# A sum kept in vector memory, carried into four matmul banks in rounded halves, and scatters that take both row halves in one step

## The chip, the cores and the metric

The kernel runs on one core of a Trainium2 chip. The metric is the device time of one execution in microseconds (us); several executions are timed and their median is given. A separate execution is recorded by the profiler, and every duration in this text comes from that one.

## The reference, cut to what matters

Two layers on 256 tokens of width 1024 in float32. The change sits at the end of the second layer, in its mixture of experts:

```
logits = xt @ w_router + b_router
top_logit, top_idx = top_k(logits, 2);  gates = softmax(top_logit)
for each token and each of its 2 experts e:
    y += gate * (silu(x @ w_gate[e]) * (x @ w_up[e])) @ w_down[e]
out = x + g_f * rms_norm(y, g_post)
```

There are 8 experts of inner width 3584. Each expert's tokens are gathered, run through three matrices, and added back to their rows with their gate weights.

## The kernel before

All weights stream once from HBM in pages of 1 MB (128 partitions by 2048 columns), issued by SyncE in a fixed order and held in a ring of buffers; a new page is issued when TensorE (PE) or VectorE (DVE) has let go of an old one.

The expert stage works on eight **units**, one for each expert. Unit 0 is a fixed expert; units 1 to 7 are the others, ranked by how many tokens they got. Unit 1 is *wide* (192 tokens: a full tile of 128 and a packed tile of 64). Units 2 and 3 hold 128 tokens. Units 4 to 7 are *narrow*, 64 tokens each. For full tiles every weight piece is split by ScalarE (ACT, line 387) and DVE (line 390) into two rounded float32 parts (type fp32r: `whi`, `wlo`), and PE multiplies three times (lines 406 to 408). For narrow tiles PE multiplies plain float32 by line 1099: the 64 tokens are the stationary operand, and the two halves of a weight row block go side by side through two column halves of the array. So the 128 partitions of a narrow unit's result hold 64 tokens twice: partitions 0 to 63 are output columns 0 to 511, partitions 64 to 127 are columns 512 to 1023. Each unit takes 7 chunks, and a chunk has three phases: gate, up, down. Each phase has four pieces. `MOE_PHASES` sets the order: units 0, 2, 3, then unit 1, with the phases of the narrow units mixed in between; from some point on only unit 7 is left.

Between pieces a phase calls `tick`, which advances one *late* generator or, when there is none, one *task* by one `yield`. A narrow phase calls it only after the last wide phase; earlier, ticks come from the full-tile phases.

**Scatter** (from line 1337) is such a late generator: when a unit's last down product is done, its result is split into fp32r halves `yr` (ACT line 387, DVE line 390), multiplied by the unit's map `PT` (line 1372) into a PSUM bank of the tag `t`, and DVE adds the bank, times the gate weight, to the running sum `acc` (line 1376). For a packed tile there are four steps, one for each of two column halves `h` and two token tiles `tt`: two matmuls of 64 rows, one DVE addition, one `yield`. The tag `t` has two banks, which the transposes of line 1190 use too.

**Unit 7** comes last and does not go to `acc`. `preload` (line 1475) has put `acc` into four PSUM banks before, through a matmul with the identity (line 1482, float32), and unit 7's scatter adds its own rows into the same banks (line 1348, float32). `closing` (line 1504) then takes the sums of squares on ACT (line 357), multiplies by the gate row on DVE (line 1510), takes the inverse root on GpSimd (line 350), does the last multiply and add on DVE (line 1515) and sends four pieces out.

Other tasks in the same tail are `gate_steps` (line 337, eight small matmuls). A branch at the end repeats work for experts whose tokens did not fit; its body does not run with this input.

Of the kernel before, what the change touches and what calls it, by code (L numbers as in the profile page):

```python
# [9 lines left out]
F32 = mybir.dt.float32  # L10
F32R = mybir.dt.float32r
BF16 = mybir.dt.bfloat16
U32 = mybir.dt.uint32
I32 = mybir.dt.int32
AF = mybir.ActivationFunctionType
# [4 lines left out]
P = 128  # L20
# [111 lines left out]
def trunk_kernel(ctx, tc, xin, cbc, sm_d, at_d, wd, wm, out, stage=9):  # L132
    nc = tc.nc
    ctx.enter_context(tc.manual_schedule())
    V, A, T, G, SY = nc.vector, nc.scalar, nc.tensor, nc.gpsimd, nc.sync
# [4 lines left out]
    tmp = ctx.enter_context(tc.tile_pool(name="tmp", bufs=2))  # L140
    ps = ctx.enter_context(tc.tile_pool(name="ps", bufs=1, space=PSUM))

    def bank(tag, bufs=1, dt=F32, shape=(P, 512)):
        return ps.tile(list(shape), dt, name=tag, tag=tag, bufs=bufs)

    def wbank():
        return bank("B", 4)
# [10 lines left out]
    def C(name):  # L158
        o, w = SM[name]
        return sm[:, o:o + w]  # L160

    ident = C("ident")
# [119 lines left out]
    plan = dense_plan()  # L282
# [13 lines left out]
    if stage >= 4:  # L296
        for u, c, w in MOE_PHASES:
            for h in range(2):
                i = c * 6 + w * 2 + h
# [53 lines left out]
    def sumsq(src_halves):  # L353
        parts = tmp.tile([P, 2], F32, name="parts", bufs=4)
        for h in range(2):
            sq = tmp.tile([P, 512], BF16, name="sq", bufs=1)
            A.activation(sq, src_halves[h], AF.Square, scale=1.0 / 32, accum_out=parts[:, h:h + 1])
        return parts

    def new_xs():  # L360
        return const.tile([P, 2, D], F32, name="xs", tag="xs", bufs=1)
# [23 lines left out]
    def split(hi, lo, v32, act=False):  # L385
        if act:
            A.activation(hi, v32, AF.Copy)  # L387
        else:
            V.tensor_copy(hi, v32)
        V.tensor_tensor(lo, v32, hi.bitcast(F32), op=ALU.subtract)  # L390
# [94 lines left out]
    for i in range(4):  # L485
# [5 lines left out]
        whole = {}  # L491
        make_hT(banks, *ab, poolH, hT, kk, True, 4, whole)
        ws.step()
        for h in range(2):
            w = ws.next("v")
            for k in kk:
                c = slice((k % 2) * 512, (k % 2) * 512 + 512)
                for tt in range(2):
                    t = slice(tt * P, tt * P + P)
# [146 lines left out]
    for i in range(16):  # L646
        w = ws.next()
        kind, j = w[2]
        b = wbank()
# [65 lines left out]
    banks, _ = finish(Y, [], stage > 1, (w[3], 4))  # L715
# [15 lines left out]
    for c in range(6):  # L731
        n = 4 if c < 5 else 2
        bs = [wbank() for _ in range(n)] if c else first + [wbank() for _ in range(2)]
# [36 lines left out]
        else:  # L770
# [4 lines left out]
            banks, _ = finish(Y, last, stage > 2)  # L775
# [97 lines left out]
    for n in range(2 * N_RNN):  # L873
# [3 lines left out]
        if n < N_RNN:  # L877
            if n == 0:
                two = [bank("y0"), bank("y1")]
                wstat_pair([b[:, :S] for b in two], [ws.next("lu") for _ in range(2)], hi, lo)  # L880
            if n < 2:
                b = two[n]
            else:
                w = ws.next("lu")
                b = wbank()
                wstat(b[:, :S], w, hi, lo)
        else:
            m = n - N_RNN
            w = ws.next("lg")
            if m % 2 == 0:  # L890
                b = gbk[m] = wbank()
# [74 lines left out]
    poolM = pa.enter_context(tc.tile_pool(name="poolM", bufs=1))  # L966
# [292 lines left out]
    class Moe:  # L1259
# [77 lines left out]
        def scatter(s, u):  # L1337


            if u.sums:  # L1340
                y = tmp.tile([P, D], F32, name="ysb", tag="yg", bufs=1)
                A.activation(y[:, :512], u.yb[0], AF.Copy)
                for _ in range(3):
                    yield
                for tt in range(2):
                    for h in range(2):
                        r = slice(64 * h, 64 * h + 64)
                        T.matmul(u.sums[tt][h], u.pt[0][r, tt * P:(tt + 1) * P], y[r, :512], start=False, stop=True)
                        yield h == 1
                return  # L1350
            if u.wide:
                ys = [[u.ya[0][:, :512], u.ya[0][:, 512:]], [u.ya[1]]]
            else:
                ys = [u.yc or u.yb]
            if s.first:
                total["acc"] = const.tile([P, 2, D], F32, name="acc", tag="xs", bufs=1)
            acc, first = total["acc"], s.first
            s.first = False
            for t, parts in enumerate(ys):
                for i, src in enumerate(parts):  # L1360
                    yr = tmp.tile([P, 2, 512], F32R, name="yr", tag="yg", bufs=1)
                    split(yr[:, 0], yr[:, 1], src, True)
                    yield
                    yield
                    whole = len(parts) == 2
                    for h in (i,) if whole else range(2):
                        q = slice(h * 512, h * 512 + 512)
                        r = slice(None) if whole else slice(64 * h, 64 * h + 64)
                        for tt in range(2):
                            b = bank("t", 2)  # L1370
                            for j in range(2):
                                T.matmul(b, u.pt[t][r, tt * P:(tt + 1) * P], yr[r, j], start=j == 0, stop=j == 1)  # L1372
                            if first:
                                V.tensor_scalar(acc[:, tt, q], b, u.weight(tt), None, op0=ALU.mult)
                            else:
                                V.scalar_tensor_tensor(acc[:, tt, q], b, u.weight(tt), acc[:, tt, q],
                                                       op0=ALU.mult, op1=ALU.add)
                            yield

        def finish(s, close):  # L1380
# [63 lines left out]
    total = {}  # L1444
# [3 lines left out]
    def quad():  # L1448
        return [(column(pr, r), 64, 0) for r in range(3, 7)]
# [6 lines left out]
    def gather_pair():  # L1456

        yield from gather(pair, [0, 1], units[2:4], taken={1: ws.pair(place[0], F32R, ("xTh", "xTl"))})
# [4 lines left out]
    plan = {  # L1463
        (0, 0, 0): [ranks(), unit0.maps()],
        (0, 4, 0): [gather_pair()],
        (2, 2, 0): [units[2].maps()],
        (3, 2, 0): [units[3].maps()],
        (0, 6, 0): [gather(quad(), [0, 1, 2, 3], units[4:8])],
        (3, 3, 2): [gather(both, [0, 1], [units[1]] * 2), lend_lo()],
        (1, 5, 0): [units[1].maps()],  # L1470
    }
# [2 lines left out]

    def preload():

        for tt in range(2):
            for h, q in enumerate(cols):
                if tt and h:
                    yield  # L1480
                b = units[7].sums[tt][h] = bank("y1") if tt and h else wbank()
                T.matmul(b, ident, total["acc"][:, tt, q], start=True, stop=False)  # L1482
                yield

    cols = [slice(0, 512), slice(512, 1024)]
    units[7].sums = [[None] * 2 for _ in range(2)]
    plan[7, 5, 1] = [preload()]
    for at, ph in enumerate(MOE_PHASES):
        if ph == (7, 3, 0):
            gate_cols(1, 5, 3)  # L1490
# [13 lines left out]
    def closing(y):  # L1504

        rs = []
        for tt in range(2):
            parts = sumsq(y[tt])
            for h, q in enumerate(cols):
                V.tensor_tensor(res[:, tt, q], y[tt][h], rows["g"][:, q], op=ALU.mult)  # L1510
            rs.append(rstd(parts))
            yield
        for tt in range(2):
            for q in cols:
                V.scalar_tensor_tensor(res[:, tt, q], res[:, tt, q], rs[tt], x[:, tt, q], op0=ALU.mult, op1=ALU.add)
                SY.dma_start(out[tt * P:(tt + 1) * P, q], res[:, tt, q])

    acc = total["acc"]
# [4 lines left out]
    with tc.If(flag > 0):  # L1523
# [14 lines left out]
        for tt in range(2):  # L1538
            r = rstd(sumsq([x[:, tt, :512], x[:, tt, 512:]]))
            for h in range(2):  # L1540
                q = slice(h * 512, (h + 1) * 512)
# [3 lines left out]
        with tc.For_i(0, N_EXP) as e:  # L1545
            V.tensor_scalar(tt8, iota8, ctr, None, op0=ALU.is_equal)
            V.tensor_scalar(ctr, ctr, 1.0, None, op0=ALU.add)
            for tt in range(2):
                for q, src in ((0, p1), (1, wt)):
                    V.tensor_tensor_reduce(jk, src[:, tt], tt8, 1.0, 0.0, op0=ALU.mult, op1=ALU.add,  # L1550
                                           accum_out=ro[:, tt, q:q + 1])
# [166 lines left out]
```

## Time and profile before

| what | value |
|---|---|
| median of 3 runs | 1429.06 us (1428.76 to 1431.05) |
| the profiled execution's own time | 1427.77 us |
| its span, first to last instruction | 1425.6 us |
| PE busy, share of the span | 97% |
| DVE, ACT busy | 63%, 49% |
| HBM rate over the span | 333 GB/s |

A row of the timeline gives the start of an instruction, its duration, engine, line, operation, output and inputs, and how many like ones were merged into it; in brackets stand the idle time of the engine ahead of it and what ended it. Matmuls overlap, so the distance between the starts of two rows tells what the first cost, not its duration. A float32 matmul shows as two rows, an fp32r one as one. "64\*128" behind a PE row is the part of the array it used, rows by columns.

### The profile page before, as it was taken

Reading aid. Unit: us, or ns where it says so; the run is one execution under the profiler, and the core shown is the slowest. Engines: PE = TensorE matmul, PEld = TensorE weight load, DVE = VectorE, ACT = ScalarE, POOL = GpSimd, SP = SyncE. Lnnn points to the kernel's source line nnn. Section 1 sums busy time; section 2 is a strip of 40 time slices with the busy share of each in tenths; the row PEclk is TensorE's granted clock in tenths of the full one; section 3 lists DMA queues with packets and bytes.
Section 4 is the critical chain, followed back from the end, with each engine's and each line's share of the span. In section 5 each row is a group of like instructions: output and inputs, shape, how many; then the busy total and the mean of one; then the engine's idle time right before and its main releaser. Section 6 shows DMA issues by size and latency. Waiting matters only on the chain.

```text
span 1425.6 us, 21512 instructions
## 1 busy us (share of the span) xinstructions
PE 1376.5 (97%) x8223; PEld 1008.6 (71%) x8223; DVE 892.1 (63%) x1269; ACT 691.9 (49%) x1022; POOL 47.8 (3%) x62
## 2 busy tenths in 40 slices
PE   5999999999898899999999999999999999999996
PEld 3796599999797678887767767766666556565652
DVE  5787598874898798988676867755332243333321
ACT  2454554444685687976655656742232232321311
POOL 0126100000000000000000000000000000000000
PEclk9999999999999999999999999999999999999999
DMA  9968498884264988699999999999999999998991
GB/s 391 385 240 318 151 349 339 338 317 192 86 240 163 364 307 307 241 344 367 384 389 416 411 389 419 391 386 408 415 400 411 393 363 401 403 409 334 387 371 60
DMA packets 76989, 476.84 MB, mean 334 GB/s; under 512 B 8528, under 2 KB 8528, under 8 KB 28880
## 3 DMA queue, kind: packets, MB, share of 16 engines
q1 hardware_dynamic: 76880, 475.40, 85.1%
q8 instruction: 66, 1.08, 0.3%
q14 instruction: 43, 0.35, 0.1%
HBM read 474.32 MB, written 1.05 MB: 333 GB/s over the span
## 4 chain that ended last, share of the span: by engine, by line
PE 55%; DVE 1%; DMA 1%; issue 0%; ACT 0%; ACTq 0%
PE B L1099 19%; PE y L1099 7%; PE B L406 7%; PE B L408 6%; PE B L407 6%; PE y L406 2%; PE y L408 2%; PE y L407 2%; PE t L1190 1%; PE t L1372 1%; DVE wlo L390 1%; DMA raw<-in_wm_dram 1%; PE t L1077 0%; PE t L1078 0%; PE B L1482 0%
## 5 line engine op out<-in xcount | busy, mean ns | idle before, releaser
L390 DVE TENSOR_TENSOR wlo<-raw,whi 128x1024 fp32r<-128x1024 f32 x451 | 541.1, 1222 | 229.2 <-ACT whi L387 193.6
L387 ACT ACTIVATE whi<-raw 128x1024 fp32r<-128x1024 f32 x448 | 464.7, 1057 | 257.7 <-PE B L408 184.2
L1099 PE MATMUL B<-raw,xTc 128*64 128x256 f32 x1792 | 205.3, 382 | 0.0
L406 PE MATMUL B<-whi,xTh 128*128 128x512 f32 x448 | 181.0, 404 | 0.0
L407 PE MATMUL B<-wlo,xTh 128*128 128x512 f32 x448 | 177.1, 395 | 0.3 <-DVE wlo L390 0.2
L1099 PEld LDWEIGHTS B<-raw,xTc 128*64 128x64 f32 x1792 | 124.3, 137 | 74.4 <-issue 16.6
L408 PE MATMUL B<-whi,xTl 128*128 128x512 f32 x448 | 176.6, 394 | 0.0
L406 PE MATMUL B<-hThi,whi 128*128 128x256 f32 x592 | 167.7, 283 | 2.0 <-ACT ge L860 1.7
L407 PE MATMUL B<-hTlo,whi 128*128 128x256 f32 x592 | 165.5, 280 | 0.0
L408 PE MATMUL B<-hThi,wlo 128*128 128x256 f32 x592 | 165.3, 279 | 0.0
L213 DVE CUSTOM_DVE_ANT_0 raw<-raw,cond 128x1024 f32<-128x1024 f32 x96 | 114.0, 1219 | 0.0
L406 PEld LDWEIGHTS B<-hThi,whi 128*128 128x128 f32 x592 | 111.2, 188 | 3.7 <-ACT ge L860 1.9
L407 PEld LDWEIGHTS B<-hTlo,whi 128*128 128x128 f32 x592 | 111.1, 188 | 0.7 <-issue 0.2
L408 PEld LDWEIGHTS B<-hThi,wlo 128*128 128x128 f32 x592 | 110.9, 187 | 0.0
L406 PEld LDWEIGHTS B<-whi,xTh 128*128 128x128 f32 x448 | 84.1, 188 | 30.6 <-issue 13.2
L1099 PE MATMUL y<-raw,hTc 128*64 128x512 f32 x448 | 101.9, 596 | 0.0
L408 PEld LDWEIGHTS B<-whi,xTl 128*128 128x128 f32 x448 | 84.1, 188 | 19.3
L407 PEld LDWEIGHTS B<-wlo,xTh 128*128 128x128 f32 x448 | 84.2, 188 | 19.2 <-DVE wlo L390 2.0
L1178 DVE TENSOR_TENSOR sg<-sg,B 128x256 f32<-128x256 f32 x35 | 14.6, 418 | 95.7 <-ACT sg L1177 95.7
L1099 PEld LDWEIGHTS y<-raw,hTc 128*64 128x64 f32 x448 | 30.6, 137 | 54.4 <-issue 52.1
L406 PE MATMUL y<-whi,hTh 128*128 128x512 f32 x168 | 67.4, 401 | 0.0
L407 PE MATMUL y<-wlo,hTh 128*128 128x512 f32 x168 | 66.4, 395 | 0.0
(329 smaller groups left out, 1681.8 us busy)
## 6 DMA issues: line engine op xcount, KB each, us to landing
raw<-in_wm_dram SPq DMA_DIRECT2D x261, 1024.0 KB, 8.7
raw<-in_wd_dram SPq DMA_DIRECT2D x114, 1024.0 KB, 6.1
raw<-in_wm_dram SPq DMA_DIRECT2D x150, 512.0 KB, 8.6
x<-in_x_dram SPq DMA_DIRECT2D x1, 1024.0 KB, 5.0
out_dram<-res SPq DMA_DIRECT2D x4, 256.0 KB, 3.0
sm<-in_sm_dram SPq DMA_DIRECT2D x1, 548.5 KB, 6.6
cond<-in_c_dram SPq DMA_DIRECT2D x1, 512.0 KB, 5.8
at<-in_at_dram SPq DMA_DIRECT2D x1, 320.0 KB, 9.6
```

The costliest lines, as they stand in the source:

```text
L213: V.tensor_tensor_reduce(src, src, cond, 1.0, 0.0, op0=ALU.mult, op1=ALU.add, accum_out=modc[:, col:col + 1])
L387: A.activation(hi, v32, AF.Copy)
L390: V.tensor_tensor(lo, v32, hi.bitcast(F32), op=ALU.subtract)
L406: T.matmul(o, lh, rh, start=start, stop=False)
L407: T.matmul(o, lh, rl, start=False, stop=False)
L408: T.matmul(o, ll, rh, start=False, stop=stop)
L1099: T.matmul(o[64 * t:64 * t + 64], xs, w[:, t * n:t * n + n], start=start, stop=stop)
L1178: V.tensor_tensor(g[t], g[t], b[:, 256:], op=ALU.mult)
L1190: T.transpose(b[:, j * P:(j + 1) * P], a[t][:, j * P:(j + 1) * P], ident)
L1372: T.matmul(b, u.pt[t][r, tt * P:(tt + 1) * P], yr[r, j], start=j == 0, stop=j == 1)
```

## The change

Three edits. In `scatter`, a packed tile's four steps of two matmuls become two steps of four: one for each token tile, with both column halves, whose matmuls alternate between partitions 0 to 63 and 64 to 127 and go to two `t` banks; DVE then adds both banks, and two yields follow. Steps of full tiles keep their order. In `preload`, each quarter of `acc` is first split into fp32r halves by ACT and DVE (the buffer `yr`, of which there is one), and two fp32r matmuls with an fp32r identity (`eye`) take the place of one float32 matmul; the generator starts one phase later and has two ticks for each quarter. In `closing`, DVE reads a row's first bank while ACT squares its second, and then the other way round.

```
-                    for h in (i,) if whole else range(2):
-                        q = slice(h * 512, h * 512 + 512)
-                        r = slice(None) if whole else slice(64 * h, 64 * h + 64)
-                        for tt in range(2):
-                            b = bank("t", 2)
-                            for j in range(2):
+                    for two in range(2):
+                        now = [(tt, i, slice(None)) for tt in range(2)] if whole else [
+                            (two, h, slice(64 * h, 64 * h + 64)) for h in range(2)]
+                        if whole:
+                            now = now[two:two + 1]
+                        bs = [bank("t", 2) for _ in now]
+                        for j in range(2):
+                            for b, (tt, h, r) in zip(bs, now):
                                 T.matmul(b, u.pt[t][r, tt * P:(tt + 1) * P], yr[r, j], start=j == 0, stop=j == 1)
+                        for b, (tt, h, r) in zip(bs, now):
+                            q = slice(h * 512, h * 512 + 512)
...
+                        yield
+                        if not whole:
                             yield
...
     def preload():
+        eye = poolM.tile([P, P], F32R, name="eye", tag="PT", bufs=4)
+        A.activation(eye, ident, AF.Copy)
         for tt in range(2):
             for h, q in enumerate(cols):
-                if tt and h:
-                    yield
+                yr = tmp.tile([P, 2, 512], F32R, name="yr", tag="yg", bufs=1)
+                split(yr[:, 0], yr[:, 1], total["acc"][:, tt, q], True)
+                yield
+                yield
                 b = units[7].sums[tt][h] = bank("y1") if tt and h else wbank()
-                T.matmul(b, ident, total["acc"][:, tt, q], start=True, stop=False)
-                yield
+                for j in range(2):
+                    T.matmul(b, eye, yr[:, j], start=j == 0, stop=False)
+        yield
...
-    plan[7, 5, 1] = [preload()]
+    plan[7, 4, 2] = [preload()]
...
-            parts = sumsq(y[tt])
+            parts = tmp.tile([P, 2], F32, name="parts", bufs=4)
             for h, q in enumerate(cols):
+                if h:
+                    square(y[tt][1], parts, 1)
+                    square(y[tt][0], parts, 0)
                 V.tensor_tensor(res[:, tt, q], y[tt][h], rows["g"][:, q], op=ALU.mult)
```

On PE, the second half of unit 6's scatter, before (`xTc` and `hTc` are narrow units' operands, `t` the shared banks, `whi` and `wlo` the split weights of unit 1):

```order
L1372 MATMUL t<-yr,PT 128x512 x2
L406 MATMUL B<-whi,hTh 128x512
L407 MATMUL B<-wlo,hTh 128x512
L408 MATMUL B<-whi,hTl 128x512
L406 MATMUL B<-whi,hTh 128x512
L407 MATMUL B<-wlo,hTh 128x512
L408 MATMUL B<-whi,hTl 128x512
L1190 MATMUL t<-sm,sg 128x128 x2
L1372 MATMUL t<-yr,PT 128x512 x2
L1099 MATMUL B<-raw,xTc 64x256 x16
L1372 MATMUL t<-yr,PT 128x512 x2
L1099 MATMUL y_11169<-raw,hTc 64x512 x8
```

and the same place now (lines have moved by 3 to 6):

```order
L411 MATMUL B<-whi,hTl 128x512
L409 MATMUL B<-whi,hTh 128x512
L410 MATMUL B<-wlo,hTh 128x512
L411 MATMUL B<-whi,hTl 128x512
L1193 MATMUL t<-sm,sg 128x128 x2
L1378 MATMUL t<-yr,PT 128x512 x4
L1102 MATMUL B<-raw,xTc 64x256 x16
L1102 MATMUL y_11169<-raw,hTc 64x512 x8
```

The step between the split pieces and the one between the two float32 phases are gone; the step behind the transposes has four matmuls.

On PE, the place of `preload` in unit 7's last phases, before (`acc` by the identity, which lies in the tile `sm`):

```order
L1099 MATMUL B<-raw,xTc 64x256 x4
L1482 MATMUL B<-acc,sm 128x512
L1099 MATMUL B<-raw,xTc 64x256 x4
L1482 MATMUL B<-acc,sm 128x512
L1099 MATMUL B<-raw,xTc 64x256 x4
L1482 MATMUL B<-acc,sm 128x512
L1099 MATMUL y_11169<-raw,hTc 64x512 x4
L1482 MATMUL y_11708<-acc,sm 128x512
L1099 MATMUL y_11169<-raw,hTc 64x512 x4
L1190 MATMUL t<-sm,sg 128x128 x2
```

and now:

```order
L1102 MATMUL y_11169<-raw,hTc 64x512 x6
L1497 MATMUL B<-yr,eye 128x512 x2
L1102 MATMUL y_11169<-raw,hTc 64x512 x2
L1193 MATMUL t<-sm,sg 128x128 x2
L1102 MATMUL B<-raw,xTc 64x256 x4
L1497 MATMUL B<-yr,eye 128x512 x2
L1102 MATMUL B<-raw,xTc 64x256 x8
L1497 MATMUL B<-yr,eye 128x512 x2
L1102 MATMUL B<-raw,xTc 64x256 x8
L1497 MATMUL y_11754<-yr,eye 128x512 x2
```

Four entries are still four, later by some pieces, and each is now two fp32r matmuls whose operands ACT and DVE must have made.

On ACT, the squares of `closing`, before (with buffer numbers; B_11683 and B_11693 are the first token tile's banks, B_11699 and y1_11708 the second's):

```order
L357 ACTIVATE sq_11780,parts_11779<-B_11683 128x512
L357 ACTIVATE sq_11782,parts_11779<-B_11693 128x512
L357 ACTIVATE sq_11793,parts_11792<-B_11699 128x512
L357 ACTIVATE sq_11795,parts_11792<-y1_11708 128x512
L1522 ACTIVATE acc_6259<-B_11683 128x512
```

and now (B_11709 and B_11726, then B_11740 and y1_11754):

```order
L361 ACTIVATE sq_11799,parts_11797<-B_11726 128x512
L361 ACTIVATE sq_11801,parts_11797<-B_11709 128x512
L361 ACTIVATE sq_11812,parts_11810<-y1_11754 128x512
L361 ACTIVATE sq_11814,parts_11810<-B_11740 128x512
L1540 ACTIVATE acc_6259<-B_11709 128x512
```

In each token tile the second bank is squared ahead of the first; DVE keeps its order, first bank and then second.

## Rows read from the trace of the kernel before

**Rows 1.** The page's first part: busy time of each engine, share of the span, instructions.

```profile
PE 1376.5 (97%) x8223; PEld 1008.6 (71%) x8223; DVE 892.1 (63%) x1269; ACT 691.9 (49%) x1022; POOL 47.8 (3%) x62
```

**Rows 2.** Waits from 1000 us to the end, the row in which PE (its weight loads, PEld) waits for a transfer: total, times, longest.

```profile
PEld y L1099 <- DMA raw<-in_wm_dram: 0.6, 2, 0.3
```

**Rows 3.** Waits of SyncE's transfer queue from 1000 us to the end, the largest row.

```profile
SPq L194 <- PE B L1099: 187.1, 120, 10.2
```

**Rows 4.** Stretches: length, busy time of PE, PEld, DVE, ACT, GpSimd, PE's granted clock, share of the DMA engines, GB/s.

```profile
1200.00:1300.00 100.00, 100.00 (x644) 61.90 (x643) 35.84 (x42) 30.60 (x42) 0.00 (x0) 1.00 1.01 406
...
1380.00:1400.00 20.00, 20.00 (x116) 8.70 (x114) 0.99 (x2) 1.96 (x4) 0.00 (x0) 1.00 0.60 218
1400.00:1426.00 26.00, 14.74 (x92) 6.38 (x88) 5.93 (x11) 6.06 (x15) 1.47 (x2) 0.86 0.12 43
```

**Rows 5.** Timeline of PE around two scatter steps of unit 6: one between unit 1's split pieces, one behind the transposes.

```profile
1299.18 0.39 PE L408 MATMUL B<-whi,hTl 128*128 128x512 f32 x1
1299.49 0.73 PE L1372 MATMUL t<-yr,PT 64*128 64x512 f32 x2
1300.16 0.50 PE L406 MATMUL B<-whi,hTh 128*128 128x512 f32 x1
1300.50 0.39 PE L407 MATMUL B<-wlo,hTh 128*128 128x512 f32 x1
1300.73 0.39 PE L408 MATMUL B<-whi,hTl 128*128 128x512 f32 x1
1300.96 0.39 PE L406 MATMUL B<-whi,hTh 128*128 128x512 f32 x1
...
1301.65 0.38 PE L1190 MATMUL t<-sm,sg 128*128 128x128 f32 x2
1302.51 0.73 PE L1372 MATMUL t<-yr,PT 64*128 64x512 f32 x2 [0.47 <-ACT hTc L1193]
```

**Rows 6.** Timeline of PE at the same place of unit 4's scatter.

```profile
986.82 0.38 PE L1190 MATMUL t<-sm,sg 128*128 128x128 f32 x2
987.13 0.74 PE L1372 MATMUL t<-yr,PT 64*128 64x512 f32 x2
```

**Rows 7.** The chain that ended last, in order of time: a float32 down phase with nothing between its pieces (start, length, what).

```profile
1290.89 3.43 PE y L1099 x16
```

**Rows 8.** Timeline of PE in the tail: steps of unit 1's packed tile between pieces of a down phase of unit 7.

```profile
1374.34 1.08 PE L1099 MATMUL y<-raw,hTc 128*64 128x512 f32 x4
1375.35 0.72 PE L1372 MATMUL t<-yr,PT 64*128 64x512 f32 x2
1376.00 1.08 PE L1099 MATMUL y<-raw,hTc 128*64 128x512 f32 x4
```

**Rows 9.** Timeline of PE: unit 7's own scatter, four float32 matmuls of 64 rows whose row halves alternate.

```profile
1413.51 1.55 PE L1348 MATMUL B<-ysb,PT 64*128 64x512 f32 x5 [0.76 <-ACT ysb L1342]
1414.48 0.59 PE L1348 MATMUL y<-ysb,PT 64*128 64x512 f32 x1
1414.90 0.59 PE L1348 MATMUL B<-ysb,PT 64*128 64x512 f32 x1
1414.91 0.59 PE L1348 MATMUL y<-ysb,PT 64*128 64x512 f32 x1
```

**Rows 10.** Timeline of DVE at unit 6's first steps.

```profile
1297.10 1.23 DVE L390 TENSOR_TENSOR wlo<-raw,whi 128x1024 fp32r<-128x1024 f32 x1 [2.04 <-ACT whi L387]
1298.24 0.74 DVE L1376 SCALAR_TENSOR_TENSOR acc<-t,wtr,acc 128x512 f32<-128x512 f32 x1
```

**Rows 11.** Timeline of PE: one identity matmul of `preload` and what follows it.

```profile
1389.96 1.13 PE L1482 MATMUL B<-acc,sm 128*128 128x512 f32 x2
1391.01 1.08 PE L1099 MATMUL B<-raw,xTc 128*64 128x256 f32 x8
```

**Rows 12.** Timeline of PE: a step of two fp32r matmuls over the whole array, between the same float32 pieces.

```profile
1365.20 0.73 PE L1372 MATMUL t<-yr,PT 128*128 128x512 f32 x2
1365.86 2.81 PE L1099 MATMUL B<-raw,xTc 128*64 128x256 f32 x24
```

**Rows 13.** Timeline of ACT behind that step: the split of the next `yr`, which waits for the buffer.

```profile
1365.97 0.64 ACT L387 ACTIVATE yr<-ya 128x512 fp32r<-128x512 f32 x1 [2.73 <-PE t L1372]
```

**Rows 14.** Timeline of DVE: the low half of the same split.

```profile
1366.63 0.69 DVE L390 TENSOR_TENSOR yr<-ya,yr 128x512 fp32r<-128x512 f32 x1
```

**Rows 15.** Timeline of ACT in `closing`: squares of the first token tile's banks.

```profile
1414.67 0.60 ACT L357 ACTIVATE sq<-B 128x512 bf16<-128x512 f32 x1 [1.21 <-PE B L1348]
1415.16 0.19 ACT L357 ACTIVATION_READ_ACCUMULATOR sq<-B 128x1 f32 x1
1415.39 0.60 ACT L357 ACTIVATE sq<-B 128x512 bf16<-128x512 f32 x1
```

**Rows 16.** Timeline of DVE in `closing`.

```profile
1415.39 1.41 DVE L1510 TENSOR_TENSOR res<-B,grow 128x512 f32<-128x512 f32 x2 [9.14 <-ACT sq L357]
1416.72 0.15 DVE L348 SCALAR_TENSOR_TENSOR var<-parts 128x1 f32<-128x1 f32 x1
1416.83 0.69 DVE L1510 TENSOR_TENSOR res<-B,grow 128x512 f32<-128x512 f32 x1
...
1418.15 0.15 DVE L348 SCALAR_TENSOR_TENSOR var<-parts 128x1 f32<-128x1 f32 x1
1418.22 2.73 DVE L1515 SCALAR_TENSOR_TENSOR res<-res,rstd,x 128x512 f32<-128x512 f32 x4
```

More of the change, by code (lines that the diff above doesn't have):

```diff
@@ L355, in sumsq, with square @@
         for h in range(2):
-            sq = tmp.tile([P, 512], BF16, name="sq", bufs=1)
-            A.activation(sq, src_halves[h], AF.Square, scale=1.0 / 32, accum_out=parts[:, h:h + 1])
-        return parts
+            square(src_halves[h], parts, h)
+        return parts
+    def square(src, parts, h):
+        sq = tmp.tile([P, 512], BF16, name="sq", bufs=1)
+        A.activation(sq, src, AF.Square, scale=1.0 / 32, accum_out=parts[:, h:h + 1])
     def new_xs():
```

## The prediction

> **What bounds the kernel now.** I read the page first: PE is busy for 97% of the span [rows 1]. A busy PE can still be one that trails its transfers, so the waits come next. From 1000 us to the end PE waits for a transfer for 0.6 us in all [rows 2], while the transfer queue waits for PE to hand buffers back, 187.1 us on line 1099 alone [rows 3]. The DMA engines are full in that time (share 1.01 at 406 GB/s) and PE as well (100.00 of 100.00 us) [rows 4]: transfers are queued as fast as PE lets go of buffers, and what they bring lies ready before PE wants it. At the end this is plain: between 1380 and 1400 the share falls to 0.60 and behind it to 0.12, which is the output, while PE has another 14.74 us of work [rows 4]. So here a microsecond of PE's queue is a microsecond of the kernel, and the terms below are distances between starts on PE, except the last, which lies behind PE's end. The clock is 1.00 up to 1400 us [rows 4], the 2.4 GHz level; the mean of 0.86 after it falls in the closing, where PE has no work.
>
> **Term A, scatters of units 4, 5 and 6.** Each loses two of its four steps. One lies between split pieces: from the last matmul ahead (start 1299.18) to the second one behind (1300.50) it is 1.32 us; without the step that is two distances of 0.23, the distance in the rows that follow, so the step costs 0.86 [rows 5]. The other lies between float32 phases. Such a step with its neighbour piece takes 1.66 (1374.34 to 1376.00) [rows 8], and a bare piece a quarter of 3.43, or 0.86 [rows 7]: 0.80. Much of either is not streaming: two matmuls at 0.23 would be 0.46.
>
> The steps that stay have four matmuls for two. Do the added ones cost anything? Unit 7's scatter is the nearest thing in the trace: float32, 64 rows, alternating halves, different banks. Its eight rows all start between 1413.51 and 1414.91, and the last two start 0.01 apart [rows 9]; one behind the other, at some 0.43 each (16 rows of 512 columns that run side by side in pairs take 3.43 [rows 7], 0.43 a pair), the last would start 3.0 us after the first, not 1.40. So row halves do run side by side. I take 0 for the added matmuls; the other bound is one after the other, 0.23 to 0.33 each (the distance in full-height rows, and half of the 0.67 from 1299.49 to 1300.16) [rows 5]. Two such for each of eight steps are 3.7 to 5.3 us.
>
> A step of both halves takes both `t` banks, hence also the one that the transposes just ahead have filled and ACT must empty. Units 5 and 6 wait for that already: 0.86 from transposes to step, 0.47 of it idle [rows 5]. Unit 4 does not, 0.31 [rows 6]; it will, for 0.55. On the other side, the transposes that follow the first wide step need a bank back: they come behind twelve split matmuls, 2.8 us, and DVE, even behind a split of 1.23, starts its first addition about 1.1 us after that split began and takes 0.7 for each [rows 10]. The splits behind the additions (`wlo`) come 0.7 us later for what unit 1 multiplies only after the narrow phases between; that hides them.
>
> A = 2 x (0.86 + 0.80) + (0.86 + 0.80 - 0.55) = 4.4 us.
>
> **Term B, unit 1's packed tile in the tail.** Two of four steps go, at 0.80 [rows 7, 8]: 1.6 us. The next step needs both banks: the additions start 0.77 behind a step's start (1365.20 to 1365.97, where ACT is let go at the same time) [rows 12, 13] and end 2 x 0.7 later, at 2.2; PE comes there after 0.66 for the step and two pieces, 1.01 and 0.86 [rows 7, 8], at 2.5. Covered, by 0.3.
>
> **Term C, the sum carried by fp32r.** An identity matmul in float32 holds its place for 1.05 us (1389.96 to 1391.01) [rows 11]; two fp32r matmuls of the same shape between the same pieces hold it for 0.66 (1365.20 to 1365.86) [rows 12]. There are four before and after: 4 x 0.39 = 1.6 us. The price is on ACT and DVE, which are idle there (0.99 and 1.96 busy in 20 us) [rows 4], and a new wait: `yr` has one buffer, so a quarter can be split only when the matmuls of the one before are through. From PE's next row (1365.86) to the end of the low half (1366.63 + 0.69) that takes 1.46 [rows 12 to 14]; PE has two pieces in between, 1.87, or a piece, transposes and a piece, over 2. What is queued behind the split on ACT is the copy of those transposes, wanted two phases later. So I take no stall. Without that cover three quarters would lose up to 1.46 each, 4.4 us.
>
> **Term D, the closing.** DVE's first multiply waits for ACT's first square of the same bank: it starts at 1415.39, 0.72 behind the square's start [rows 15, 16]. Now the two engines start on different banks at 1414.67 and swap. Each half takes 0.7 on either engine, a square with its read-out 0.72 [rows 15]. So the first tile's squares and products end at about 1416.1, `var` starts there instead of at 1416.72, and the second tile needs 1.5 more: its `var` at 1417.7, not 1418.15, and the last four operations start 0.47 earlier than 1418.22 [rows 16]. They run back to back and the output follows them. D = 0.5 us, between 0 and the 0.72 of the first wait.
>
> **The sum.** 4.4 + 1.6 + 1.6 + 0.5 = 8.1 us. The profiled execution's own 1427.77 becomes 1419.7 and its span 1425.6 becomes 1417.5; it lies 1.3 below the median of the runs, 1429.06, so the median becomes 1421.0.
>
> **Rivals.** (1) Row halves overlap only in part, or not for fp32r. Rows 9 speak against it, but they are float32. One after the other the gain is 8.1 less 3.7 to 5.3: 1424.7 to 1426.3.
>
> By the Trainium skill, page "TensorE: Matmul & The Clock Gate", section "Measured speedup vs the span model", four row tiles of 512 columns ran 3.07 times as fast as one after the other, not 4 times. If two tiles lost the same share, an estimate is some 0.13 us for each of eight steps and 1422.1 for the kernel; rows 9, with their last two starts 0.01 apart, show no such loss.
>
> (2) The transfers take PE's gain back. The DMA engines are at 1.01 [rows 4], so a PE that asks faster isn't fed faster; if nothing lay ready, A would be lost and B to D, behind the last transfers or nearly, would stay: 1429.06 - 3.7 = 1425.4. Against it stand 0.6 us of waits in 426 us and a queue that waits for PE [rows 2, 3]: what lies ready covers 4.4 us over 400.
>
> (3) Slower: the double step starves the tag `t`. Both its banks are held until DVE has done two additions in a row, and DVE takes its work in order. If a split of 1.23 comes ahead of them [rows 10] and the next user stands directly behind, it waits for this and for the additions, some 2.4 us. From 1.0 us for each of the eight steps the whole gain is gone; at 2.4 in six steps and 1.2 in two the kernel ends 8.7 us slower, at 1437.8. Against it speaks the cover worked out under A and B; it fails only if that cover isn't there.
>
> (4) The change doesn't do what it says. On PE the order of instructions shows four double steps for eight and four fp32r entries for four, so this remains for the closing alone, and costs 0.5 us.
>
> **How the numbers follow.** Forecast, all terms within 1.5 us of their sum: 0.72, at 1421.0. Rival 1: 0.13. Rival 2: 0.10. Rival 3 to the full: 0.03; rival 3 in part, so that it eats most of the gain: 0.02. A measurement of this kernel can tell about 0.2%, 2.9 us, from no change, so faster means under 1426.2. The forecast, rival 2 and most of rival 1 are there: 0.93. The rest of rival 1 and the partial case give no change: 0.04; slower 0.03. The range: at its low end the wait of unit 4 is hidden (0.55) and D is 0.72, and the runs fall 0.3 below their median as the lowest before does, 1.1 in all; the eight steps cost 0.1 more each than I read, 0.8: 1421.0 - 1.9 is 1419.1, and I say 1419.0. At its high end stands rival 2 and the nearer part of rival 1: 1425.4.
>
> **What would show it.** In the trace of the changed kernel line 1378 must have its double steps with pairs of starts within 0.02 us and still some 0.66 to the next row; if a second pair starts 0.46 or more behind the first, rival 1 holds. Entries of line 1497 must hold their place for about 0.66, with no idle time put down to DVE's `yr`. PE's waits for transfers must stay near 0.6 us; several us on line 1102 or on ACT's `whi` with PE idle behind it mean rival 2. Idle time ahead of transposes or double steps put down to DVE's `acc` is rival 3. In the closing DVE's first product and ACT's first square must start together. The prediction is wrong if the gain lies under 4 us, and its reasons are wrong if it isn't spread over the four terms.

## The result, and the profile after

The changed kernel takes 1419.94 us (median of 4 runs, 1419.24 to 1420.95), the kernel before beside it 1429.13: a ratio of 0.9939, with a 95% interval of 0.9928 to 0.9951. The prediction was 1421.0 us within 1419.0 to 1425.4.

The profiled execution of the changed kernel is the slowest of its four, 1420.95 us with a span of 1419.0, so the two spans differ by 6.6 us and the medians by 9.2. Part of this lies ahead of the change: unit 4's first scatter step starts at 982.39 us before and at 983.61 after, though the order of work up to there is the same in both. I therefore compare from that step on: 443.25 us to the end before, 435.38 after, so 7.87 us less. The changed kernel was profiled a second time, below, and the stretch took 435.63, so it repeats within some 0.3 us, while its beginning wanders from 981.8 to 985.5 in the runs told of here.

By the page's first part PE is busy for 1371.4 us in the changed kernel, 5.1 less than before, with as many instructions, 8223 [rows 1]. They are the same in number because a float32 matmul and two fp32r ones both count as two.

The stretches that answer to [rows 4] (length, then busy time of PE, PEld, DVE, ACT, GpSimd, granted clock, DMA share, GB/s):

```profile
1200.00:1300.00 100.00, 100.00 (x646) 61.96 (x644) 37.43 (x44) 31.27 (x43) 0.00 (x0) 1.00 1.01 404
1380.00:1400.00 20.00, 20.00 (x136) 9.98 (x134) 3.61 (x6) 4.35 (x9) 0.00 (x0) 1.00 0.42 158
```

PE is full in both, at 2.4 GHz (1.00), as before; ACT and DVE do more in the second, the splits of the sum. From 960 us to the end, the waits of PE's weight loads (PEld) for transfers and for DVE's additions, and the largest row of the transfer queue:

```profile
PEld t L1193 <- DVE acc L1384: 0.8, 1, 0.8
...
PEld t L1378 <- DVE acc L1384: 0.8, 1, 0.8
...
PEld y L1102 <- DMA raw<-in_wm_dram: 0.6, 2, 0.3
...
PEld B L1102 <- DMA raw<-in_wm_dram: 0.4, 1, 0.4
```

```profile
SPq L194 <- PE B L1102: 199.9, 131, 9.4
```

PE waits 1.0 us for transfers in 459, 0.6 before [rows 2]; the 0.4 more lies at 977 us, ahead of the first changed step. The transfer queue still waits for PE, 199.9 us on this line in 459 us for 187.1 in 426 [rows 3]. Two weight loads wait for DVE's additions, 0.8 us each, where rival 3 needed whole microseconds at most of the steps, and the kernel before has two like them in the same stretch:

```profile
PEld t L1372 <- DVE acc L1376: 0.8, 1, 0.8
PEld t L1190 <- DVE acc L1376: 0.8, 1, 0.8
```

So rivals 2 and 3 didn't come about.

Now the places of the terms. PE at unit 6, where [rows 5] were read:

```profile
1295.66 0.74 PE L1378 MATMUL t<-yr,PT 64*128 64x512 f32 x4
1296.33 0.50 PE L409 MATMUL B<-whi,hTh 128*128 128x512 f32 x1
...
1299.23 0.38 PE L1193 MATMUL t<-sm,sg 128*128 128x128 f32 x2
1299.54 1.27 PE L1378 MATMUL t<-yr,PT 64*128 64x512 f32 x4
1300.74 3.67 PE L1102 MATMUL B<-raw,xTc 128*64 128x256 f32 x32
1304.24 3.60 PE L1102 MATMUL y<-raw,hTc 128*64 128x512 f32 x16
```

The first step has four matmuls and holds its place for 0.67 us (1295.66 to 1296.33), as two did (1299.49 to 1300.16 in [rows 5]). How many of them are in flight is seen in short stretches, of this line alone:

```profile
1295.66:1295.67 0.01, 0.01 (x2) 0.01 (x2) 1.00 5.84 2458
...
1296.00:1296.02 0.02, 0.02 (x4) 0.00 (x0) 1.00 1.48 614
```

Two start within the first 0.01 us, and by 1296.02 the other two are under way as well. The second double step starts 0.31 us behind the transposes and holds its place for 1.20 (1299.54 to 1300.74): its later matmuls can't start until ACT has emptied the transposes' bank by copying it to `hTc`, so the wait is inside the step. It shows as idle time of the weight loads, here from 1295 to 1305 us:

```profile
PEld t L1378 <- ACT hTc L1196: 0.4, 1, 0.4
```

From transposes to the next phase it is 1.51 us, in units 4, 5 and 6 alike; before it was 1.52 for unit 6 too (1301.65, then 0.86 to the step and 0.66 for it), with half the matmuls.

PE in the tail, unit 1's packed tile and two entries of `preload`:

```profile
1370.45 0.74 PE L1378 MATMUL t<-yr,PT 64*128 64x512 f32 x4
1371.11 1.94 PE L1102 MATMUL y<-raw,hTc 128*64 128x512 f32 x8
1372.98 0.72 PE L1378 MATMUL t<-yr,PT 64*128 64x512 f32 x4
1373.63 1.08 PE L1102 MATMUL y<-raw,hTc 128*64 128x512 f32 x4
...
1387.49 0.73 PE L1497 MATMUL B<-yr,eye 128*128 128x512 f32 x2
1388.15 1.08 PE L1102 MATMUL y<-raw,hTc 128*64 128x512 f32 x4
...
1390.54 0.73 PE L1497 MATMUL B<-yr,eye 128*128 128x512 f32 x2
```

An entry holds its place for 0.66 (1387.49 to 1388.15), and no idle time is put down to DVE's `yr`. DVE, the low half of the second quarter's split and then the closing:

```profile
1388.92 0.69 DVE L393 TENSOR_TENSOR yr<-acc,yr 128x512 fp32r<-128x512 f32 x1 [2.06 <-ACT yr L390]
...
1408.32 1.45 DVE L1528 TENSOR_TENSOR res<-B,grow 128x512 f32<-128x512 f32 x2 [8.36 <-PE B L1351]
...
1411.47 2.73 DVE L1533 SCALAR_TENSOR_TENSOR res<-res,rstd,x 128x512 f32<-128x512 f32 x4
```

The half split is done at 1389.61, and PE wants it at 1390.54: 0.9 us of cover. In the closing the first product waits for PE's last matmuls and no longer for ACT, whose first square starts 0.04 behind it:

```profile
1408.36 0.60 ACT L361 ACTIVATE sq<-B 128x512 bf16<-128x512 f32 x1 [1.25 <-PE B L1351]
```

Each term by distances between starts (us), from the PE timelines of both traces, the closing's end from DVE's:

| stretch | before | after | change | forecast |
|---|---|---|---|---|
| A, unit 4: first step to the next down phase | 14.08 | 12.99 | -1.09 | -1.11 |
| A, unit 5 | 10.19 | 8.58 | -1.61 | -1.66 |
| A, unit 6 | 10.18 | 8.58 | -1.60 | -1.66 |
| B: down phase with the packed tile, to the next phase | 6.99 | 5.52 | -1.47 | -1.60 |
| C: from there to the last 24 rows of the last down phase | 27.67 | 26.08 | -1.59 | -1.56 |
| D: from there to DVE's last four operations | 10.84 | 10.38 | -0.46 | -0.47 |
| sum | | | -7.82 | -8.06 |

### The profile page after: what moved, and what is told of

The parts are those of the page before. It is cut to its first block, busy times and chain, and to the rows that moved or that the text cites. A ratio compares the mean times of both kernels' runs of the same rounds, so it can differ in the third digit from the quotient of the medians.

```text
span 1419.0 us, 21522 instructions
## 1 busy us (share of the span) xinstructions
PE 1371.4 (97%) x8223; PEld 1008.4 (71%) x8223; DVE 894.5 (63%) x1273; ACT 694.5 (49%) x1027; POOL 47.8 (3%) x62
## 4 chain that ended last, share of the span: by engine, by line
PE 55%; DVE 1%; DMA 1%; issue 0%; ACT 0%; ACTq 0%
PE B L1102 19%; PE y L1102 7%; PE B L409 7%; PE B L411 6%; PE B L410 6%; PE y L409 2%; PE y L410 2%; PE y L411 2%; PE t L1193 1%; PE t L1378 1%; DVE wlo L393 1%; DMA raw<-in_wm_dram 1%; PE t L1080 0%; PE t L1081 0%; PE B L337 0%
```

## The experiments

The kernels of one group ran on the same chip beside the kernel before (1428.46, 1428.26 and 1428.38 us for the first four, the next four and the last two). Two numbers are given for each: the median, and the stretch from unit 4's first step to the end (443.25 before, 435.38 in the changed kernel), which shows differences too small for the median. Much of what does not repeat in the stretch lies at its end: with the same closing, the part from the start of unit 7's scatter on takes 11.58 to 12.10 us in these profiles. Up to that start the two profiles of the changed kernel take 423.55 and 423.62 us, and this shorter stretch is given where the end blurs a difference.

**One edit alone, three times.** First the scatters (terms A and B) with `preload` and `closing` as before; then `preload` alone; then `closing` alone. The code of each edit is as in the diff ahead.

> The kernel before with the scatter edit alone. Theory (each step taken out of PE's queue gives its whole place back, and PE sets the end): the stretches read from the two traces give 4.3 us for units 4 to 6 and 1.5 us for unit 1's packed tile, so the median falls by 5.8 us, to 1423.3. Rival (the transfers take back what is won ahead of the tail): only the 1.5 us of the tail stay, 1427.6.

Measured: 1422.76 us, ratio 0.9964 (0.9951 to 0.9978); the stretch is 437.30, so 5.95 less than before, where A and B together were forecast at 6.0. The recorded rival, 1427.6, falls, and so does the one in which the halves run one after the other.

> The kernel before with the preload edit alone. Theory: four entries at 0.66 us of PE for four at 1.05, no wait for the split: 1.6 us less, 1427.5. Rival (the split of a quarter is late for its matmuls): up to 4.4 us of idle PE ahead of line 1497's matmuls, so 1427.5 to 1432.

Measured: 1426.10 us, ratio 0.9983 (0.9974 to 0.9992), the stretch 441.35, 1.90 less. The four entries hold their place for 0.65 to 0.66 us each. It gives C, and by 0.3 us more than C; the distance from unit 7's scatter to the end, which this edit doesn't touch, was shorter by 0.25 in this run (1411.69 to 1423.57 against 1413.51 to 1425.64). Up to that scatter it is 1.65 less.

> The kernel before with the closing edit alone. Theory: the first product starts with the first square, the last four operations start 0.45 us earlier, 1428.7, which the runs can hardly tell from no change, so the trace decides: from the last down phase's start to the last operations 10.4 us for 10.8. Rival (ACT is the later engine either way): 10.8.

Measured: 1427.11 us, ratio 0.9994 (0.9985 to 1.0003): by the median alone it can't be told from no change. The trace can. DVE's closing in this kernel:

```profile
1416.06 1.46 DVE L1516 TENSOR_TENSOR res<-B,grow 128x512 f32<-128x512 f32 x2 [8.41 <-PE B L1351]
...
1419.22 2.73 DVE L1521 SCALAR_TENSOR_TENSOR res<-res,rstd,x 128x512 f32<-128x512 f32 x4
```

There the first product waits for PE. In the kernel with the scatters alone, whose closing is that of before, it waits for ACT's square:

```profile
1409.25 1.41 DVE L1517 TENSOR_TENSOR res<-B,grow 128x512 f32<-128x512 f32 x2 [9.14 <-ACT sq L357]
...
1412.08 2.74 DVE L1522 SCALAR_TENSOR_TENSOR res<-res,rstd,x 128x512 f32<-128x512 f32 x4
```

From the start of unit 7's scatter (1414.90 and 1407.37) to the last four operations it is 4.32 us with the edit and 4.71 without, as before (1413.51 to 1418.22): 0.39. The stretch is 442.84, so 0.41 less. The three gains sum to 5.95 + 1.90 + 0.41 = 8.26, the whole change gave 7.87, so the edits add up to within the run-to-run spread.

**The alternating order of row halves.** The change puts the matmuls of a double step in alternating order. Here both matmuls of one half come ahead of both of the other:

```
-                        for j in range(2):
-                            for b, (tt, h, r) in zip(bs, now):
+                        for b, (tt, h, r) in zip(bs, now):
+                            for j in range(2):
                                 T.matmul(b, u.pt[t][r, ...], yr[r, j], ...)
```

> The changed kernel, but within a double step both matmuls of one row half come ahead of both of the other. Theory (the halves overlap because they alternate): PE takes instructions in order, so only the middle pair can overlap, and each of eight steps takes 0.23 us longer: 1.9 us more, 1421.8. Rival (the halves overlap in any order, the gain is the number of steps alone): no change, 1419.9. Second rival (nothing overlaps in this order): 0.46 each, 3.7 us more, 1423.6.

Measured: 1420.11 us, ratio 0.9944 (0.9931 to 0.9958), the stretch 435.92 against 435.38. Unit 6's first step on PE, and the matmuls in flight in it:

```profile
1294.53 0.74 PE L1378 MATMUL t<-yr,PT 64*128 64x512 f32 x4
1295.20 0.50 PE L409 MATMUL B<-whi,hTh 128*128 128x512 f32 x1
```

```profile
1294.53:1294.54 0.01, 0.01 (x2) 0.01 (x2) 1.00 0.00 0
...
1294.87:1294.89 0.02, 0.02 (x4) 0.00 (x0) 1.00 0.51 205
```

The step holds its place for 0.67 us again, and again two are in flight at once. Two matmuls of one half were 0.34 us apart in the kernel before, so by the records this pair is one of each half, and the one of the second half stands third in PE's order. My expectation fell: row halves overlap in either order, and the alternation is worth at most the 0.3 to 0.5 us by which the stretch is longer, not 1.9; up to unit 7's scatter it is 423.83, 0.2 to 0.3 longer. The step behind the transposes takes 1.19 (1298.41 to 1299.60) against 1.20.

**The cover of the split.** One tick for each quarter of `preload` where the change has two:

```
                 split(yr[:, 0], yr[:, 1], total["acc"][:, tt, q], True)
                 yield
-                yield
```

> The changed kernel with one tick in place of two between the split of a quarter of the sum and its two matmuls; nothing is left out of the computation. Theory (the cover of term C is what hides the split): from PE's next row to the end of the split's low half 1.46 us are needed, and one piece covers 0.86 to 1.01, so each of the last three quarters waits 0.45 to 0.6 us, PE shows idle time put down to DVE's yr on the preload's line, and the kernel takes 1.3 to 1.8 us longer than the changed one (1421.2 to 1421.7 against 1419.9). Rival (the split is hidden with far less, since ACT and DVE are idle there, or the splits are as fast as one piece): no idle time on that line, 1419.9, and four preload steps of 0.66 each as now.

Measured: 1419.49 us, ratio 0.9939 (0.9925 to 0.9952), the stretch 435.56. PE at the four entries:

```profile
1384.85 0.78 PE L1496 MATMUL B<-yr,eye 128*128 128x512 f32 x2
1385.56 1.08 PE L1102 MATMUL y<-raw,hTc 128*64 128x512 f32 x4
1386.57 1.00 PE L1496 MATMUL B<-yr,eye 128*128 128x512 f32 x2
1387.50 1.08 PE L1102 MATMUL y<-raw,hTc 128*64 128x512 f32 x4
1388.51 0.44 PE L1193 MATMUL t<-sm,sg 128*128 128x128 f32 x2
1388.71 0.81 PE L1496 MATMUL B<-yr,eye 128*128 128x512 f32 x2
...
1390.46 0.99 PE L1496 MATMUL y<-yr,eye 128*128 128x512 f32 x2
1391.39 6.26 PE L1102 MATMUL B<-raw,xTc 128*64 128x256 f32 x56
```

and at the second split, DVE and the weight load of the second matmul:

```profile
1386.33 0.69 DVE L393 TENSOR_TENSOR yr<-acc,yr 128x512 fp32r<-128x512 f32 x1 [1.26 <-ACT yr L390]
```

```profile
1387.08 0.19 PEld L1496 LDWEIGHTS B<-yr,eye 128*128 128x128 f32 x1 [0.32 <-DVE yr L393]
```

The wait is there, but it is small: an entry starts on time on the half that ACT has written, and its second matmul waits for DVE's, done at 1387.02. It is idle time of the weight loads, 0.3 us in two entries, put down to DVE's `yr` as expected; PE's matmuls themselves show none. These two entries hold their place for 0.93 where 0.66 is the rule. An entry that stands right behind the transposes saves 0.17 there (transposes to the next row 0.20, not 0.37). In all the tail from the phase ahead to unit 7's scatter takes 25.34 us (1380.39 to 1405.73) where the changed kernel took 24.99 (1382.17 to 1407.16): 0.35 lost, where I expected 1.3 to 1.8.

**The wait behind the transposes.** A third tick after a packed tile's first double step, so that the second stands between two float32 phases:

```
                        if not whole:
                            yield
+                            if not two:
+                                yield
```

> The changed kernel with one more tick behind the first double step of a packed tile, so that the second one stands between two float32 phases of the narrow unit and not directly behind the transposes; nothing is left out of the computation. Theory (the 0.55 us wait is for the transposes' bank, inside the double step, in units 4, 5 and 6): from transposes to the next float32 row falls from 1.51 to about 0.37 us, the double step costs 0.80 in its new place, so each of the three units gains 0.34 us and the kernel 1.0: 1418.9. Rival (the float32 phase behind the transposes needs ACT's copy of the same bank anyway, so that the wait only moves from the step to the phase): no gain, or 0.3 to 0.5 us lost for each unit, 1419.9 to 1421.4.

Measured: 1418.66 us, ratio 0.9930 (0.9916 to 0.9943), the stretch 434.53, 0.85 less than the changed kernel's. PE at unit 6:

```profile
1300.37 0.38 PE L1193 MATMUL t<-sm,sg 128*128 128x128 f32 x2
1300.68 3.67 PE L1102 MATMUL B<-raw,xTc 128*64 128x256 f32 x32
1304.29 0.73 PE L1378 MATMUL t<-yr,PT 64*128 64x512 f32 x4
1304.95 3.65 PE L1102 MATMUL y<-raw,hTc 128*64 128x512 f32 x16
```

The float32 phase doesn't wait for the transposes' bank: it starts 0.31 us behind them. From unit 6's first step to the down phase it is now 8.14 (1296.81 to 1304.95), not 8.58, and units 4 and 5 gain as much (12.56 and 8.15 for 12.99 and 8.58). But unit 1's second step has moved behind transposes too, and takes 1.20 there (1374.95 to 1376.15): its stretch is 5.92 instead of 5.52. So 3 x 0.43 - 0.40 = 0.9.

**Fewer switches, without row halves.** Steps of full tiles too take both token tiles at once:

```
                        now = [(tt, i, slice(None)) for tt in range(2)] if whole else [
                            (two, h, slice(64 * h, 64 * h + 64)) for h in range(2)]
-                        if whole:
-                            now = now[two:two + 1]
+                        if whole and two:
+                            yield
+                            continue
```

> The changed kernel in which full tiles too take their two steps (one for each token tile) as one step of four matmuls followed by an empty tick; nothing is left out of the computation. These matmuls use all 128 rows, so they can't run side by side; only the switches between float32 and fp32r neighbours are saved. Theory (a step's cost above its streaming is two switches): unit 1's full tile in the tail has four steps between float32 pieces, each 0.66 for 0.46 of streaming, and they become two of 0.66 + 0.46, which saves 2 x 0.2 = 0.4, with the piece's own part of the switch up to 0.7; units 0, 2 and 3 have fp32r neighbours and gain nothing: 1419.2 to 1419.5, below what the rounds can tell, so the trace of the tail decides. Rival (the gain of the packed tile came from the row halves alone, not from fewer switches): four matmuls in one step take as long as two steps, and the tail keeps its length.

Measured: 1420.88 us, ratio 0.9943 (0.9930 to 0.9957), the stretch 434.40, 0.98 less than the changed kernel's; the median doesn't show it. PE in the tail, unit 1's full tile:

```profile
1360.97 1.08 PE L1102 MATMUL B<-raw,xTc 128*64 128x256 f32 x8
1361.99 1.20 PE L1379 MATMUL t<-yr,PT 128*128 128x512 f32 x4
1363.11 3.67 PE L1102 MATMUL B<-raw,xTc 128*64 128x256 f32 x32
...
1370.49 1.03 PE L1102 MATMUL y<-raw,hTc 128*64 128x512 f32 x4
```

Four matmuls over all rows hold their place for 1.12 us, two hold it for 0.66: the two added ones cost 0.46, their streaming, and the rest of a step is paid once. The phase takes 9.52 (1360.97 to 1370.49) where the changed kernel took 10.29 (1359.20 to 1369.49), 0.77 less. The stretch's other 0.2 lies behind unit 7's scatter: up to there it is 422.76, 0.8 less than the changed kernel's.

So part of a step's price is paid at its two ends. My expectation put it down to the change between float32 and fp32r; the rows of the kernel before say that it is the part of the array that changes. There a full-tile step between split pieces has neighbours of its own type on its own part of the array:

```profile
962.18 0.40 PE L408 MATMUL B<-whi,xTl 128*128 128x512 f32 x1
962.41 0.63 PE L1372 MATMUL t<-yr,PT 128*128 128x512 f32 x2
962.88 0.39 PE L406 MATMUL B<-whi,xTh 128*128 128x512 f32 x1
```

It costs 0.47 (962.41 to 962.88), its streaming alone. The packed step between split pieces is fp32r among fp32r as well, but it uses 64 rows where they use 128, and it cost 0.86 for 0.46 [rows 5]. And where the type changes but the part does not, nothing is lost: from a split matmul to the float32 transposes on the whole array the distance stays 0.23 (three distances in the 0.69 from 1300.96 to 1301.65) [rows 5]. In unit 1's tail type and part change together.

Two such merges give 0.39 each; the two of the packed tile in the same tail gave 1.47, or 0.73 each. By that difference, an estimate, about half of what a merge brings there is due to row halves that run side by side.

**Both, and then the better form of both.**

> The two edits before this one together in one kernel: a third tick behind a packed tile's first double step, and full tiles' steps in pairs; nothing is left out of the computation. By theory their gains add up, 1.0 and 0.4 to 0.7: 1418.2 to 1418.5, the fastest of all kernels here. Rival: if either turns out to be without gain, this one shows the other alone.

Measured: 1418.95 us, ratio 0.9931 (0.9917 to 0.9944), the stretch 433.72, 1.66 less than the changed kernel's: 0.85 and 0.98 nearly add up. Up to unit 7's scatter they do: 422.78 and 422.76 for the single edits, 422.00 for both. The last form gives the third tick to units 4 to 6 alone (`if not two and t == 0`), and the changed kernel ran again beside it:

> Both edits of the kernel before this one, but the third tick only for units 4 to 6, since in unit 1 it moved the second double step behind transposes and cost 0.40 us there (5.92 against 5.52 from the last float32 piece ahead of the first step to the next phase); nothing is left out of the computation. Theory (each edit is worth what its place on PE shows): three units gain 0.43 each and the full tile's pairs 0.77, 2.1 us less than the changed kernel, so that the stretch from unit 4's first step to the end takes 433.3 us where the changed kernel's took 435.4, and unit 1's packed tile 5.52 again. Rival (what PE gains behind 980 us comes back as waits for transfers once it is large enough): the stretch stays at the 433.7 of the kernel before this one or above.

> The changed kernel again, unaltered, beside the run before it on the same chip and beside the kernel before. Theory (its four terms as the trace shows them, 7.8 us; the 9.2 of its first runs was partly chance): 7.8 us below the kernel before, a ratio of 0.9945, and again 435.4 us within 0.3 from unit 4's first step to the end, wherever the earlier part of the run ends. Rival (something in the code ahead of unit 4 got faster too): 9 us or more, a ratio of 0.9936 or less, and a first step of unit 4 that starts 1 us or more ahead of the 982.0 to 983.8 of the runs so far.

Measured: 1418.66 us (1417.48 to 1420.75), ratio 0.9929 (0.9915 to 0.9942), for the last form, and 1420.52 (1419.36 to 1421.10), ratio 0.9941 (0.9928 to 0.9955), for the changed kernel. The stretches are 433.18 and 435.63, against 433.3 and 435.4 expected. In the last form unit 1's packed tile stands as in the changed kernel:

```profile
1369.28 1.03 PE L1102 MATMUL y<-raw,hTc 128*64 128x512 f32 x4
...
1374.80 1.08 PE L1102 MATMUL B<-raw,xTc 128*64 128x256 f32 x8
```

From 1369.28 to 1374.80 it is 5.52 again. So this is the fastest kernel here by the trace, 2.2 to 2.5 us ahead of the changed one, and 1.9 to 2.0 up to unit 7's scatter (421.61), where 2.1 was expected; its median is 1.9 below, with intervals of the two ratios that overlap.

## Why the prediction was right

**The bound.** A microsecond off PE's queue behind 980 us was a microsecond off the kernel. The six places gave 7.82 us and the stretch that holds them 7.87; the kernel with scatters alone gave 5.95 of 6.0. What PE gained didn't come back as a wait for transfers, not even in the last form, whose stretch is 2.2 us shorter still. Rival 2 is out for gains of this size.

**Term A** held within 0.13 us: 4.30 for 4.43. The added matmuls cost nothing. The step that the prediction chose for its rows, the float32 one of unit 7 [rows 9], was a fair sign for fp32r. From the speedup of 3.07 that the Trainium skill, page "TensorE: Matmul & The Clock Gate", section "Measured speedup vs the span model", gives for four row tiles, the prediction had an estimate of 0.13 us lost in each double step. The trace doesn't agree: a double step holds its place for the 0.67 us of a single one. Unit 4's new wait has its size, 0.54 for 0.55: from its transposes to the next phase it is 0.97 us before and 1.51 after. But it sits inside the step, on the second half's bank, and not ahead of it as the prediction had it.

**Term B** was 0.13 too large. I took 0.80 for both steps that went. One of them stood behind transposes before and held its place for 0.66 only (1379.05 to 1379.71), and 0.80 + 0.66 is 1.46, with 1.47 measured.

**Term C** held: 1.59 for 1.56, and 1.9 us for the edit alone. The cover was there, with more to spare than I claimed: the 1.46 us behind PE's next row are those of the low half, which only an entry's second matmul needs; the high half is there 0.74 behind that row (1385.56 to 1385.67 + 0.63 in the run with one tick). So the price that I named for no cover at all, 4.4 us, was somewhat high. From these rows, an estimate: with no cover an entry's second matmul would start some 1.5 us behind PE's row and the next row 0.42 later (1387.08 to 1387.50), so an entry would lose 1.3 and three 3.8. No run leaves out all of the cover.

**Term D** held in the trace, 0.46 for 0.47. DVE's first product and ACT's first square start 0.04 us apart, as said.

**The size in all.** The traces say 7.8 us and the forecast said 8.1. The median fell by 9.2 in the first comparison and by 7.9 in the second (1428.38 to 1420.52), and both intervals hold 7.8. Nothing ahead of unit 4 was shown to be faster, so the 1.4 us beyond 7.8 in the first comparison are taken for chance; that isn't shown. Why one execution reaches unit 4 up to 3.7 us later than another is settled only in part: PE's granted clock goes with it. Over the first 500 us it is 0.98 in four of the profiles, the changed kernel's first among them, and 0.99 in the other eight; part of that time it stands at the 1.2 GHz level. The four reach unit 4 at 983.6 to 985.5 us, the others at 981.8 to 983.5, but for one at 985.4. The runs say the same: of the 39 executions of the kernel before that ran beside the experiments, the 11 with a mean granted clock of 0.989 or 0.990 took 1429.3 to 1432.6 us, the 28 with 0.992 to 0.995 took 1426.9 to 1430.9. From 980 to 1400 us it is 1.00 in all twelve profiles, so this does not touch the stretch that the terms are read from.

## What to carry to other kernels

Where the tensor engine is the bound and its queue mixes kinds of work, count the places at which its matmuls move to another part of the array, and not only the columns: a step of two matmuls cost 0.66 to 0.86 us for 0.46 of streaming where the part changed, and 0.47 where it stayed, and taking two such steps as one saved 0.39 us even where the matmuls can't overlap. A step that needs a buffer just filled by other work should stand one phase later; here that gave 0.43 us in each of three units. For differences below a few tenths of a per cent, compare a stretch between two fixed instructions of the traces, once it has been seen to repeat, leave out an end that does not, and leave the median to say that nothing else has moved.

## What the hardware showed that I had not expected

By the records, a matmul of the other row half started within 0.01 us of the first although one of the first half stood between them in the order. I had expected PE to go strictly by the order here, and the times to follow. The two halves of a split are waited for one by one: with one tick of cover an entry started on time on the first half and lost 0.27 us inside (0.93 for 0.66), shown as idle time of the weight loads and not of PE's matmuls. And a change of the part of the array costs time where the type stays fp32r (0.86 for 0.46), while a change from fp32r to float32 on the same part costs none (0.23, as between split matmuls).
